# The opening modulation: weight pages become the stationary operand of the product

## The chip, the cores and the metric

The kernel runs on one core of a Trainium2 chip. The time is device microseconds of one execution, lower is better. Before the change three timed runs gave 2663.68, 2665.32 and 2666.12 us, so the median is 2665.32 us.

A core has TensorE (matrix products; PE in the profile, and PEld for its weight loads), VectorE (DVE), ScalarE (ACT), GpSimd (POOL) and SyncE (SP), whose queue issues the transfers between HBM and on-chip memory. A product on TensorE has a stationary operand, which a load brings into the array, and a moving operand, whose columns pass through it.

## The reference

One layer of a hybrid diffusion backbone works on 1024 latent tokens and 256 context tokens of width 1024. Each sublayer normalizes its tokens and modulates them with vectors that come from a conditioning vector through one weight matrix, `w_ada` (1024 x 9216). Latent tokens are conditioned on `c`, context tokens on `c_ctx`:

```python
mods   = split(silu(c) @ w_ada + b_ada, 9)
mods_c = split(silu(c_ctx)[None] @ w_ada + b_ada, 9)
h  = ffn_sublayer(h,  mods[0],   mods[1],   mods[2],   g_ffn1, w_ffn1_in, w_ffn1_out)
hc = ffn_sublayer(hc, mods_c[0], mods_c[1], mods_c[2], g_ffn1, w_ffn1_in, w_ffn1_out)

def ffn_sublayer(h, shift, scale, gate, g, w_in, w_out):
    hn = rmsnorm(h, g) * (1 + scale) + shift
    a, b = split(hn @ w_in, 2)
    return h + 0.5 * gate * ((silu(a) * b) @ w_out)
```

Behind these come the projections, a bidirectional mLSTM, a spatial gating unit, the merge, a second feed-forward sublayer for the latent tokens, and a last RMSNorm. The change touches only the first two modulations, shift and scale (columns 0 to 2047 of `w_ada`), for both conditions.

## The kernel before

Everything is kept transposed: features on the 128 partitions, tokens along the free dimension. Width 1024 is eight blocks of 128 features, called d. Big products use pairs of fp32r pages: a value is split into a rounded high part (a copy on ScalarE) and a residue (a subtraction on VectorE), and the product is made of three terms. `split` (L175) does this for weight pages. A product of plain fp32 operands appears in the trace as two loads and two matmuls.

The opening, up to about 51 us, works in this order. `ada_page` (L859) loads the 2048 columns of `w_ada` as sixteen pages of 512 KB: four quarters `qt` of 2 x 256 columns (shift and scale), with four pages `kp` each, and two blocks k of 128 inputs in each page. All transfers are issued on SyncE's queue, in the order of the loop from L938: the sixteen pages, with the two halves of the context tokens `hcp` after the second and the fourth, the first raw feed-forward page (`W.fetch`, tile `wraw`) after the fourteenth, three more raw pages at the end, then constants, and later eight more raw pages, which take the buffers of the pages of quarters 0 and 1, and the latent tokens (`h`).

`ada_mm` (L864) multiplies one page. The stationary operand is the conditioning (four columns: both conditions, as high parts and residues or with two zero columns) and the page moves, 512 columns at a time. Of every four blocks one goes as plain fp32 (L869), and three are split into `adhi` (ScalarE, L872) and `adlo` (VectorE, L874) and multiplied in two fp32r products (L875, L876). A quarter's result is a row of 512 values on four partitions; `ada_out` (L878) copies it and turns it into columns with four small fp32 products (L883), so that features lie on partitions. `ada_mods` (L886) adds the bias and makes scale factors.

Between the pages stand the sums of squares of the context tokens (`sums_c`, L962), the reciprocal root (`rstd_c`), its broadcast (`bcast_c`, L979), and per quarter `mod_a` (scale, tile `nt`, VectorE, L991) and `mod_b` (shift and split, tile `hnc`, ScalarE L996 and VectorE L997), which finish two of the eight blocks d of the modulated context tokens.

`tile0` (L1001) splits one raw feed-forward page into `hl`, and `proj_k` (L953) multiplies it with blocks of `hnc`, three fp32r matmuls of 256 columns for each block: 24 for a tile of 128 output features. The first three tiles are made in the opening, tile by tile as `hnc` gets ready; from L1076 a loop makes the remaining ones in pairs, gates them (`gate_c`) and stores them, while latent tokens are loaded and normalized in the background. `Weights` (L130) holds four split pages; `done` splits the next raw page and fetches another.

The order on TensorE, ScalarE and VectorE is fixed by hand: inside `inorder(last0)` each instruction is made to follow the one before it on its engine, and the loop that follows pins TensorE in the same way. Ten products of a page of ones (`WARM`, L1009) run before the first page is there.

Of the kernel before, what the change touches and what calls it, by code (L numbers as in the profile page):

```python
# [9 lines left out]
F32 = mybir.dt.float32  # L10
F32R = mybir.dt.float32r
# [27 lines left out]
NVEC = _o  # L39


WARM = 10
COST = lambda f: getattr(f, 'cost', 512)
MODG = lambda d: d % 2 == 0

# [12 lines left out]
def _build(ctx, tc, nc, a, out):  # L58
# [39 lines left out]
    def t2(name, dt=F32, shape=(128, 512)):  # L98
        return tp.tile(list(shape), dt, name=name, tag="t2", bufs=12)

    def mm_ps(name):
        return ps.tile([128, 512], F32, name=name, tag="mm", bufs=4)

    def sm_ps(name):
        return ps.tile([128, 512], F32, name=name, tag="sm", bufs=4)
# [679 lines left out]
    S.activation(sc2[:, 0, :], vs_("c"), AF.Silu)  # L785
    S.activation(sc2[:, 1, :], vs_("c_ctx"), AF.Silu)
    mods = cp.tile([128, 9, 2, 8], F32, name="mods")
    c4 = cp.tile([128, 8, 4], F32R, name="c4")
    cz = cp.tile([128, 16, 4], F32, name="cz")[:, :8]
    G.memset(cz, 0.0)  # L790
    ck = sc2.rearrange("p q k -> p k q")
    S.copy(c4[:, :, 0:2], ck)
    V.tensor_sub(c4[:, :, 2:4], ck, c4[:, :, 0:2].bitcast(F32))
    V.tensor_copy(cz[:, :, 0:2], ck)
    pick = t2("pick", shape=(4, 2))
    V.tensor_add(pick, ident[0:4, 0:2], ident[0:4, 2:4])

    def ada_load(page, m, hf, k):
        pgt = page()
# [54 lines left out]
    NQ = 4  # L854
# [4 lines left out]
    def ada_page(qt, kp):  # L859
        pg = hnp.tile([128, KP, 2, QW], F32, name="adapg", tag=f"pg{1 - qt // 2}", bufs=8)  # L860
        nc.sync.dma_start(pg.rearrange("p k m c -> p (k m c)"), a["w_ad0"][qt * (NKT // KP) + kp])
        return pg

    def ada_mm(pages, pr, kp):  # L864
        for j in range(KP):
            k = kp * KP + j
            src = pages[kp][:, j].rearrange("p m c -> p (m c)")
            if k % 4 == 0:
                T.matmul(pr[0:4, :], cz[:, k, :], src, start=k == 0, stop=False, skip_group_check=True)  # L869
                continue  # L870
            hi = t2("adhi", F32R)
            S.copy(hi, src)  # L872
            lo = t2("adlo", F32R)
            V.tensor_sub(lo, src, hi.bitcast(F32))  # L874
            T.matmul(pr[0:4, :], c4[:, k, :], hi, start=False, stop=False, skip_group_check=True)  # L875
            T.matmul(pr[0:2, :], c4[:, k, 0:2], lo, start=False, stop=k == NKT - 1, skip_group_check=True)  # L876

    def ada_out(qt, pr):  # L878
        row = t2("adrow", shape=(4, 2 * QW))
        S.copy(row, pr[0:4, :])  # L880
        pc = sm_ps("adc")
        for i in range(2 * QD):
            T.matmul(pc[:, 2 * i:2 * i + 2], row[:, i * 128:(i + 1) * 128], pick, start=True, stop=True)  # L883
        return pc

    def ada_mods(qt, pc):  # L886
        sl = slice(qt * QD, (qt + 1) * QD)
        bv = vs_("b_ada").rearrange("p (m d) -> p m d", m=9)
        for m in range(2):
            V.tensor_add(mods[:, m, :, sl],  # L890
                         pc[:, m * 2 * QD:(m + 1) * 2 * QD].rearrange("p (d q) -> p q d", q=2),
                         bv[:, m:m + 1, sl].to_broadcast([128, 2, QD]))
        V.scalar_tensor_tensor(smod[:, 0, :, sl], mods[:, 1, :, sl], 1.0,
                               vs_("g_ffn1")[:, sl].unsqueeze(1).to_broadcast([128, 2, QD]), ALU.add, ALU.mult)
# [43 lines left out]
    apg = [[] for _ in range(NQ)]  # L938
    for qt in range(NQ):
        for kp in range(NKT // KP):  # L940
            apg[qt].append(ada_page(qt, kp))
            if qt == 0 and kp % 2:
                i = kp // 2
                nc.sync.dma_start(hcp[i], a["cT"][4 * i:4 * i + 4].rearrange("d p t -> p d t"))
            if (qt, kp) == (3, 1):
                W.fetch(wfirst)
    for _ in range(3):
        W.fetch(wfirst)
    nc.sync.dma_start(cst[:, 1:], a["cst"].rearrange("p (a b) -> p a b", a=5)[:, 1:])
    nc.sync.dma_start(pos, a["pos"])  # L950
# [11 lines left out]
    def sums_c(p4, ds):  # L962
        for d in ds:
            sq = [t2("sq")[:, :256] for _ in range(2)]
            for i in range(2):
                S.activation(sq[i], hc[d + i], AF.Square)
            V.tensor_add(sq[0], sq[0], sq[1])
            for j in range(2):
                T.matmul(p4[:, j:j + 1], sq[0][:, j * 128:(j + 1) * 128], ones[:, 0:1], start=d == 0 and j == 0,
                         stop=d == NKT - 2, skip_group_check=True)  # L970

    def rstd_c(p4):
        y = rsqrt(p4[:, :2], 2, 1.0 / D)
        diag = t2("diag")
        for j in range(2):
            V.tensor_scalar(diag[:, j * 128:(j + 1) * 128], ident, y[:, j:j + 1], None, ALU.mult)
        return diag

    def bcast_c(diag):  # L979
        rb = sm_ps("rb")  # L980
        T.matmul(rb[:, :256], ones, diag[:, :256], start=True, stop=True)
        return rb[:, :256]
# [2 lines left out]
    nts = {}  # L985

    def mod_a(qt):
        ada_mods(qt, adc.pop(0))
        for d in range(qt * QD, (qt + 1) * QD):
            nts[d] = t2("nt")[:, :256]  # L990
            V.scalar_tensor_tensor(nts[d], hc[d], scc[:, d:d + 1], rsc, ALU.mult, ALU.mult)  # L991
# [9 lines left out]
    def tile0():  # L1001
        W.load()
        first.append(W.take("w1i", len(first)))
        pf.append(mm_ps("pa")[:, :256])

    last0 = {}
    with inorder(last0):
        wps = sm_ps("wps")
        for i in range(WARM):  # L1009
            T.matmul(wps[:, :128], ones, ones, start=True, stop=True)  # L1010
        pr = sm_ps("adr")
        for kp in range(4):
            ada_mm(apg[0], pr, kp)
        p4 = sm_ps("p4")
        sums_c(p4, (0, 2))
        for qt in range(1, NQ):
            pq, pr = pr, sm_ps("adr")
            ada_mm(apg[qt], pr, 0)
            if qt == 1:
                sums_c(p4, (4, 6))  # L1020
            elif qt == 2:
                mod_a(0)
            adc.append(ada_out(qt - 1, pq))
            ada_mm(apg[qt], pr, 1)
            if qt == 1:
                dg = rstd_c(p4)
            else:
                if qt == 2:
                    mod_b(0)
                mod_a(qt - 1)  # L1030
            ada_mm(apg[qt], pr, 2)
            if qt == 1:
                rb_ = bcast_c(dg)
            ada_mm(apg[qt], pr, 3)
            if qt == 1:
                S.copy(rsc, rb_)
            else:
                mod_b(qt - 1)
        tile0()
        proj_k(pf[0], first[0], range(4))  # L1040
        adc.append(ada_out(3, pr))
        tile0()
        proj_k(pf[0], first[0], (4, 5))
        mod_a(3)
        proj_k(pf[1], first[1], range(6))
        mod_b(3)
        tile0()
        proj_k(pf[0], first[0], (6, 7))
        proj_k(pf[1], first[1], (6, 7))
        W.load()  # L1050
        proj_k(pf[2], first[2], range(NKT))

    for _ in range(W.ahead):
        W.fetch(wraw)
    for i in range(3):
        W.done(wraw)

    n1 = [Norm(h[tb], 512, V) for tb in range(2)]
# [17 lines left out]
    for f in range(NF):  # L1076
        if f < NKT:
            for tb in range(2):
                nc.sync.dma_start(h[tb][f], a["xT"][f, :, tb * 512:(tb + 1) * 512])
        if 2 <= f < 2 + NKT:  # L1080
            for tb in range(2):
                slow(add_pos, tb, f - 2, cost=512, later=True)
                slow(n1[tb].sq, f - 2, cost=512, later=True)
                slow(nc.sync.dma_start, hsp[tb, f - 2], h[tb][f - 2], cost=0)
        if f == 2 + NKT:
            todo.extend([n1[0].rstd, n1[1].rstd] + [nop] * 12 + [n1[0].bcast, n1[1].bcast] + [nop] * 4)
            for d in range(4):
                slow(n1[0].inplace, d, s0, b0, cost=512, later=True)
                slow(A.F.early, fpage, 1, d, cost=512, later=True)
        if f == 12:  # L1090
            A.head()
        if f > 12:
            A.preload()
        if f == NF - 1:
            A.q.ring = lambda: hnpage(1, "ring0")
            for _ in range(HEAD):
                A.q.load()
            A.q.ring = A.ring
        if f:
            if f == 1:  # L1100
                pa = pf[2]
            else:
                pa = mm_ps("pa")[:, :256]
                proj(pa, W.take("w1i", 2 * f), hnc)
            gated()
            if f > 1:
                W.done(wraw)
            pb = mm_ps("pb")[:, :256]
            proj(pb, W.take("w1i", 2 * f + 1), hnc)
            W.done(wraw)  # L1110
        else:
            pa, pb = pf[0:2]
        gated = it(gate_c, f, pa, pb)
# [1164 lines left out]
```

## Time and profile before

| what | value |
|---|---|
| median of three timed runs | 2665.32 us (2663.68 to 2666.12) |
| profiled execution, its own time | 2660.64 us |
| span of its trace | 2658.8 us |
| TensorE busy | 2634.2 us, 99% of the span |
| mean granted TensorE clock | 0.998 |
| first modulation product starts | 5.85 us |
| last modulation product starts | 36.86 us |
| fifth projection tile starts | 51.19 us |

The trace is one execution on the chip. A line of the timeline gives start and length in microseconds, engine, line of the kernel, operation, output and inputs by the program's names, shape and count, and in brackets the idle time of the engine before it with what ended it. A line of the groups gives the busy time and the mean length of one. Matmuls are pipelined, so their lengths overlap, and the distance between starts is what a product costs. The granted clock is the share of full speed that TensorE was given.

### The profile page before, as it was taken

The page shows a single profiled execution, that of the slowest core. Times are in us where ns is not written, and L with a number is a line of the kernel's source. Part 1 is how long each engine was busy: PE and PEld are TensorE (multiplying, and loading weights), DVE is VectorE, ACT ScalarE, POOL GpSimd, SP SyncE. Part 2 cuts the span into 40 slices and gives each one's busy share as a digit, 9 for nine tenths or more (in the row PEclk, how much of TensorE's full clock was granted, in tenths as well). Part 3 has the DMA queues.
Part 4 walks back from the last instruction along what each step waited for, and adds up shares of the span by engine and source line. Part 5 has one row for each costly group of instructions (what it writes and reads, how often), then busy time and mean ns, then how long its engine had stood idle before and what let it go on. Part 6 is the DMA issues. An engine that isn't in the chain of part 4 may idle for free.

```text
span 2658.8 us, 35689 instructions
## 1 busy us (share of the span) xinstructions
PE 2634.2 (99%) x12766; PEld 2207.2 (83%) x12766; DVE 2018.3 (76%) x3633; ACT 1095.3 (41%) x1883; POOL 124.2 (5%) x211
## 2 busy tenths in 40 slices
PE   9999999999999999999999999999999999999998
PEld 6998888888889878888888888888887888888887
DVE  7889889788879647788774878677568877776855
ACT  6664333334346525554443342111345433334432
POOL 0000000000000000000000005342000000000000
PEclk9999999999999999999999999999999999999999
DMA  9923444369568122256553477448240433337545
GB/s 376 328 90 127 167 138 159 125 216 324 170 222 293 65 88 86 100 182 206 189 176 110 133 253 264 158 161 280 76 142 32 153 123 135 116 119 276 184 161 171
DMA packets 193090, 456.76 MB, mean 172 GB/s; under 512 B 20240, under 2 KB 40464, under 8 KB 192912
## 3 DMA queue, kind: packets, MB, share of 16 engines
q1 hardware_dynamic: 192912, 454.47, 50.4%
q8 instruction: 101, 1.65, 0.2%
q14 instruction: 77, 0.63, 0.1%
HBM read 328.95 MB, written 125.51 MB: 171 GB/s over the span
## 4 chain that ended last, share of the span: by engine, by line
PE 89%; DVE 5%; DMA 2%; issue 2%; ACT 1%; SPq 0%; POOL 0%; POOLq 0%; DVEq 0%; ACTq 0%
PE qb L431 20%; PE po L557 15%; PE pq L1427 13%; PE qa L431 10%; PE pt L1901 9%; PE pr L1338 6%; PE pb L206 2%; PE pc L1209 2%; PE pa L206 2%; PE pn L2014 2%; PE pu L1740 2%; PE pkc L1407 1%; PE pn L2012 1%; DVE ring L175 1%; PE pvc L1498 1%
## 5 line engine op out<-in xcount | busy, mean ns | idle before, releaser
L175 ACT CAST ring<-rawq 128x512 fp32r<-128x512 f32 x432 | 265.8, 620 | 533.2 <-PE qb L431 188.4
L557 PE MATMUL po<-gring,wring 128*128 128x512 f32 (+1 forms) x1896 | 425.0, 385 | 0.4 <-DMA gring<-fsp 0.4
L557 PEld LDWEIGHTS po<-gring,wring 128*128 128x128 f32 x1896 | 349.7, 188 | 71.5 <-issue 1.5
L175 DVE TENSOR_TENSOR ring<-rawq,ring 128x512 fp32r<-128x512 f32 x432 | 296.0, 689 | 131.5 <-ACT ring L175 130.1
L431 PE MATMUL qb<-fc,ring 128*128 128x512 f32 x1440 | 339.7, 390 | 0.1
L431 PEld LDWEIGHTS qb<-fc,ring 128*128 128x128 f32 x1440 | 270.2, 188 | 56.6 <-DVE u L452 0.8
L431 PE MATMUL qa<-fa,ring 128*128 128x512 f32 x1056 | 253.0, 390 | 0.0
L431 PEld LDWEIGHTS qa<-fa,ring 128*128 128x128 f32 x1056 | 198.2, 188 | 41.4 <-issue 0.5
L431 PE MATMUL qb<-fb,ring 128*128 128x512 f32 x984 | 229.8, 390 | 0.0
L431 PEld LDWEIGHTS qb<-fb,ring 128*128 128x128 f32 x984 | 184.7, 188 | 38.3
L1427 PE MATMUL pq<-fc,ring 128*128 128x512 f32 x864 | 211.1, 393 | 0.3 <-DVE py L1440 0.2
L1427 PEld LDWEIGHTS pq<-fc,ring 128*128 128x128 f32 x864 | 161.0, 188 | 33.8 <-DVE py L1440 1.4
L175 ACT CAST wring<-rw 128x512 fp32r<-128x512 f32 x154 | 95.9, 622 | 225.9 <-PE po L557 197.2
L1901 PE MATMUL pt<-yp,ring 128*128 128x512 f32 x768 | 184.3, 397 | 0.0
L175 DVE TENSOR_TENSOR wring<-rw,wring 128x512 fp32r<-128x512 f32 x154 | 105.6, 685 | 93.3 <-ACT wring L175 93.0
L1901 PEld LDWEIGHTS pt<-yp,ring 128*128 128x128 f32 x768 | 144.2, 188 | 29.2
L1427 PE MATMUL pq<-fa,ring 128*128 128x512 f32 x576 | 139.8, 391 | 0.0
L1427 PE MATMUL pq<-fb,ring 128*128 128x512 f32 x576 | 137.3, 393 | 0.0
L1427 PEld LDWEIGHTS pq<-fb,ring 128*128 128x128 f32 x576 | 107.7, 188 | 22.2 <-PE pu L1781 0.3
L1427 PEld LDWEIGHTS pq<-fa,ring 128*128 128x128 f32 x576 | 107.3, 188 | 21.8 <-DVE ring L175 0.2
L175 ACT CAST ring<-rawt 128x512 fp32r<-128x512 f32 x64 | 39.7, 620 | 187.6 <-PE pt L1901 177.5
L813 DVE SCALAR_TENSOR_TENSOR adacc<-adapg,sc,adacc 128x512 f32<-128x512 f32 x140 | 102.6, 745 | 8.3 <-DMA adapg<-in_w_ada_dram 7.5
(367 smaller groups left out, 4112.3 us busy)
## 6 DMA issues: line engine op xcount, KB each, us to landing
fsp<-fhl SPq DMA_DIRECT2D x66, 512.0 KB, 2.7
gring<-fsp SPq DMA_DIRECT2D x66, 512.0 KB, 3.4
adapg<-in_w_ada_dram SPq DMA_DIRECT2D x112, 256.0 KB, 3.5
wraw<-in_w1i_dram SPq DMA_DIRECT2D x44, 512.0 KB, 5.5
graw<-fsp SPq DMA_DIRECT2D x88, 256.0 KB, 3.4
rawq<-in_w1i_dram SPq DMA_DIRECT2D x38, 512.0 KB, 4.2
rawq<-in_w2i_dram SPq DMA_DIRECT2D x38, 512.0 KB, 3.3
fsp<-x SPq DMA_DIRECT2D x66, 256.0 KB, 2.0
```

The lines of the kernel that those rows point to most:

```text
L175: ins = S.copy(hl[:, 0, :], src).ins, V.tensor_sub(hl[:, 1, :], src, hl[:, 0, :].bitcast(F32)).ins
L206: T.matmul(pt, x, y, start=i == 0, stop=i == n - 1)
L431: T.matmul(pt, hl[:, x, sl], pages[p][k][:, y, :], start=first and i == 0, stop=i == 11, skip_group_check=not first)
L557: T.matmul(pt[:, cs], w[:, x, sl], g[:, y, cs], start=grp and kp == 0 and i == 0, stop=kp == NFP - 1 and i == 2, skip_group_check=not grp)
L813: eng.scalar_tensor_tensor(acc, pgt, sc2[:, q, k:k + 1], acc, ALU.mult, ALU.add)
L1209: T.matmul(pt, hl[d // 4][:, x, sl], g[:, y, :], start=f == 0 and d % 2 == 0 and i == 0, stop=f == NF - 1 and i == 2, skip_group_check=True)
L1338: T.matmul(self.pt[m], pg[:, x, sl], hl[:, y, :], start=first and k == 0 and i == 0, stop=k == 3 and i == 2, skip_group_check=not first)
L1407: T.matmul(self.cp[:, o:o + 256], hl[:, x, k * 128:(k + 1) * 128], hnc[kc][:, y, :], start=p == 1 and k == 0 and i == 0, stop=p in (2, 4) ...
L1427: T.matmul(pt, hl[:, x, k * 128:(k + 1) * 128], pg[k][:, y, :], start=first and k == 0 and i == 0, stop=k == 3 and i == 2, skip_group_chec ...
L1740: T.matmul(pu[:, 0:257], ksl[:, kt * 128:(kt + 1) * 128], wv, start=True, stop=True)
L1901: T.matmul(pt, hl[:, x, k * 128:(k + 1) * 128], pg[:, y, :], start=kh + k + i == 0, stop=kh == 1 and k == 3 and i == 2)
L2014: T.matmul(pn[:, 0:257], qi[:, c_, :], self.C[d][:, c_, :], start=False, stop=c_ == 1)
```

## The change

The operands change places. Each 128 x 128 block of a page, in plain fp32, is now the stationary operand, and the conditioning moves: both conditions and thirty columns of zeros, 32 columns. The result comes out with features on partitions, so the row copy and the turning products go, as do the splits of the pages. A quarter makes 32 products (eight blocks k, four blocks of output features), which accumulate in one PSUM tile.

The order changes with it. Token halves are loaded ahead of the first and the second page, and one raw feed-forward page after every quarter. The sums of squares run within quarter 0, the modulation of a quarter follows it at once and is followed by a `tile0`; projection columns (`cols`) stand after the second page of quarters 1, 2 and 3, and a fourth tile is made in the opening. The warm-up has sixteen products instead of ten. A spare tile `gap_` takes the place of a removed one.

```diff
-WARM = 10
+WARM = 16
...
-    c4 = cp.tile([128, 8, 4], F32R, name="c4")
-    cz = cp.tile([128, 16, 4], F32, name="cz")[:, :8]
+    gap_ = cp.tile([128, 32], F32, name="gap_")
+    cz = t2("cz")[:, 0:256].rearrange("p (k n) -> p k n", k=8)
     G.memset(cz, 0.0)
-    ck = sc2.rearrange("p q k -> p k q")
-    S.copy(c4[:, :, 0:2], ck)
-    V.tensor_sub(c4[:, :, 2:4], ck, c4[:, :, 0:2].bitcast(F32))
-    V.tensor_copy(cz[:, :, 0:2], ck)
-    pick = t2("pick", shape=(4, 2))
-    V.tensor_add(pick, ident[0:4, 0:2], ident[0:4, 2:4])
+    V.tensor_copy(cz[:, :, 0:2], sc2.rearrange("p q k -> p k q"))
...
-    def ada_mm(pages, pr, kp):
+    NC = 32
+
+    def ada_mm(qt, kp, pr):
         for j in range(KP):
             k = kp * KP + j
-            src = pages[kp][:, j].rearrange("p m c -> p (m c)")
-            if k % 4 == 0:
-                T.matmul(pr[0:4, :], cz[:, k, :], src, start=k == 0, stop=False, skip_group_check=True)
-                continue
-            hi = t2("adhi", F32R)
-            S.copy(hi, src)
-            lo = t2("adlo", F32R)
-            V.tensor_sub(lo, src, hi.bitcast(F32))
-            T.matmul(pr[0:4, :], c4[:, k, :], hi, start=False, stop=False, skip_group_check=True)
-            T.matmul(pr[0:2, :], c4[:, k, 0:2], lo, start=False, stop=k == NKT - 1, skip_group_check=True)
-
-    def ada_out(qt, pr):
...
+            for i in range(2 * QD):
+                m, d = divmod(i, QD)
+                T.matmul(pr[:, NC * i:NC * i + NC], apg[qt][kp][:, j, m, d * 128:(d + 1) * 128], cz[:, k, 0:NC],
+                         start=k + i == 0, stop=k == NKT - 1, skip_group_check=True)
...
     for qt in range(NQ):
         for kp in range(NKT // KP):
+            if qt == 0 and kp < 2:
+                nc.sync.dma_start(hcp[kp], a["cT"][4 * kp:4 * kp + 4].rearrange("d p t -> p d t"))
             apg[qt].append(ada_page(qt, kp))
-            if qt == 0 and kp % 2:
-                i = kp // 2
-                nc.sync.dma_start(hcp[i], a["cT"][4 * i:4 * i + 4].rearrange("d p t -> p d t"))
-            if (qt, kp) == (3, 1):
-                W.fetch(wfirst)
-    for _ in range(3):
         W.fetch(wfirst)
...
+        for qt in range(NQ):
+            adc.append(sm_ps("adc"))
+            for kp in range(4):
+                ada_mm(qt, kp, adc[qt])
+                if (qt, kp) == (0, 0):
+                    p4 = sm_ps("p4")
+                    sums_c(p4, (0, 2))
+                elif (qt, kp) == (0, 1):
+                    sums_c(p4, (4, 6))
+                    dg = rstd_c(p4)
+                elif (qt, kp) == (0, 3):
+                    S.copy(rsc, bcast_c(dg))
+                    mod_a(0)
+                    mod_b(0)
+                    tile0()
+                elif (qt, kp) == (1, 1):
+                    cols(0, 0, 1)
+                elif (qt, kp) == (2, 1):
+                    cols(0, 2, 3)
+                    cols(1, 0, 1, 2, 3)
+                elif (qt, kp) == (3, 1):
+                    cols(2, 0, 1, 2, 3)
+            if qt:
+                mod_a(qt)
+                mod_b(qt)
+                tile0()
+        for i in range(3):
+            cols(i, 4, 5)
+        for i in range(3):
+            cols(i, 6, 7)
+        cols(3, *range(NKT))
...
-    for i in range(3):
+    for i in range(4):
         W.done(wraw)
...
             if f == 1:
-                pa = pf[2]
+                pa, pb = pf[2:4]
+                gated()
```

More of the change, by code (lines that the diff above doesn't have):

```diff
@@ L862, in ada_page @@
         return pg
-    def ada_mm(pages, pr, kp):
+    NC = 32
+    def ada_mm(qt, kp, pr):
         for j in range(KP):
             k = kp * KP + j
-            src = pages[kp][:, j].rearrange("p m c -> p (m c)")
-            if k % 4 == 0:
-                T.matmul(pr[0:4, :], cz[:, k, :], src, start=k == 0, stop=False, skip_group_check=True)
-                continue
-            hi = t2("adhi", F32R)
-            S.copy(hi, src)
-            lo = t2("adlo", F32R)
-            V.tensor_sub(lo, src, hi.bitcast(F32))
-            T.matmul(pr[0:4, :], c4[:, k, :], hi, start=False, stop=False, skip_group_check=True)
-            T.matmul(pr[0:2, :], c4[:, k, 0:2], lo, start=False, stop=k == NKT - 1, skip_group_check=True)
-    def ada_out(qt, pr):
[L879 to L884, printed above, removed]
+            for i in range(2 * QD):
+                m, d = divmod(i, QD)
+                T.matmul(pr[:, NC * i:NC * i + NC], apg[qt][kp][:, j, m, d * 128:(d + 1) * 128], cz[:, k, 0:NC],
+                         start=k + i == 0, stop=k == NKT - 1, skip_group_check=True)
     def ada_mods(qt, pc):
@@ L890, in ada_mods @@
             V.tensor_add(mods[:, m, :, sl],
-                         pc[:, m * 2 * QD:(m + 1) * 2 * QD].rearrange("p (d q) -> p q d", q=2),
+                         pc[:, m * NC * QD:(m + 1) * NC * QD].rearrange("p (d q) -> p q d", q=NC)[:, 0:2, :],
                          bv[:, m:m + 1, sl].to_broadcast([128, 2, QD]))
@@ L987, in mod_a @@
     def mod_a(qt):
-        ada_mods(qt, adc.pop(0))
+        ada_mods(qt, adc[qt])
         for d in range(qt * QD, (qt + 1) * QD):
@@ L1004, in tile0, with cols @@
         pf.append(mm_ps("pa")[:, :256])
+    def cols(i, *ks):
+        proj_k(pf[i], first[i], ks)
     last0 = {}
@@ L1010, in _build @@
             T.matmul(wps[:, :128], ones, ones, start=True, stop=True)
[L1011 to L1028, printed above, removed]
-                    mod_b(0)
[L1030 to L1051, printed above, removed]
+        for qt in range(NQ):
[11 more added lines that the diff above has]
+                    mod_a(0)
+                    mod_b(0)
+                    tile0()
[10 more added lines that the diff above has]
+                tile0()
@@ L1104, in _build @@
                 proj(pa, W.take("w1i", 2 * f), hnc)
-            gated()
-            if f > 1:
+                gated()
                 W.done(wraw)
-            pb = mm_ps("pb")[:, :256]
-            proj(pb, W.take("w1i", 2 * f + 1), hnc)
-            W.done(wraw)
+                pb = mm_ps("pb")[:, :256]
+                proj(pb, W.take("w1i", 2 * f + 1), hnc)
+                W.done(wraw)
         else:
```

## The prediction

> **What bounds the kernel now.** I read the page's busy table first, then the chain of waits over the first 100 us, then TensorE's timeline and the stage table of that stretch, and last the groups by shape and the queue's issues.
>
> ```profile
> span 2658.8 us, 35689 instructions
> PE 2634.2 (99%) x12766; PEld 2207.2 (83%) x12766; DVE 2018.3 (76%) x3633; ACT 1095.3 (41%) x1883; POOL 124.2 (5%) x211
> ```
>
> TensorE is busy over the whole span, so time can only move where its work or its waits change: the opening. The profiled execution took 2660.64 us, 1.84 us more than its span; the median of the timed runs is 2665.32 us, 4.7 us above it. I make the sum in the profile's time and add the difference it gives to the median.
>
> TensorE's timeline of the opening (start, length, instructions, and what ended an idle time):
>
> ```profile
> 0.97 4.03 PE L1010 MATMUL wps<-ones 128*128 128x128 f32 x20 [0.97 <-POOL epst L88]
> 5.85 1.02 PE L869 MATMUL adr<-adapg,cz 128*4 128x512 f32 x2 [0.85 <-DMA adapg<-in_w_ad_dram]
> ...
> 13.47 1.20 PE L969 MATMUL p<-ones,sq 128*128 128x1 f32 x8
> ...
> 18.41 1.05 PE L883 MATMUL adc<-pick,adrow 4*128 4x2 f32 x8
> ...
> 29.54 0.40 PE L876 MATMUL adr<-adlo,c 128*2 128x512 f32 x1 [0.98 <-DVE adlo L874]
> 29.77 0.40 PE L875 MATMUL adr<-adhi,c 128*4 128x512 f32 x1
> ...
> 31.06 1.02 PE L869 MATMUL adr<-adapg,cz 128*4 128x512 f32 x2
> 32.01 0.40 PE L875 MATMUL adr<-adhi,c 128*4 128x512 f32 x1
> ...
> 36.86 0.40 PE L876 MATMUL adr<-adlo,c 128*2 128x512 f32 x1
> ...
> 38.79 1.45 PE L957 MATMUL pa<-hnc,hl 128*128 128x256 f32 x10 [1.30 <-DVE hl L175]
> ...
> 48.35 3.00 PE L206 MATMUL pb<-hnc,hl 128*128 128x256 f32 x24
> 51.19 3.00 PE L206 MATMUL pa<-hnc,hl 128*128 128x256 f32 x24
> ```
>
> The first page is used at 5.85, the last modulation product starts at 36.86, and 51.19 is my mark: there the fourth projection tile of the context tokens is done and the fifth starts. From then on tile follows tile every 2.84 us (51.19 - 48.35) with no idle time, before and after the change alike. What the change is worth is how far this mark moves.
>
> Who paces the stretch up to 36.86 is in the groups of the first 52 us (count, busy us, mean ns, idle before) and in the transfer rates:
>
> ```profile
> L874 DVE TENSOR_TENSOR adlo<-adapg,adhi 128x512 fp32r<-128x512 f32 x24 | 15.6, 687 | 7.7 <-ACT adhi L872 7.7
> L872 ACT CAST adhi<-adapg 128x512 fp32r<-128x512 f32 x24 | 13.7, 614 | 6.0 <-DMA adapg<-in_w_ad_dram 5.9
> L175 DVE TENSOR_TENSOR hl<-wraw,hl 128x1024 fp32r<-128x1024 f32 x7 | 8.3, 1222 | 0.6 <-ACT hl L175 0.5
> L175 ACT CAST hl<-wraw 128x1024 fp32r<-128x1024 f32 x8 | 8.2, 1043 | 2.5 <-issue 1.2 <-PE pa L957 1.2
> L991 DVE SCALAR_TENSOR_TENSOR nt<-hc,smod,rsc 128x256 f32<-128x256 f32 x8 | 3.5, 482 | 0.2
> L997 DVE SCALAR_TENSOR_TENSOR hnc<-nt,mods,hnc 128x256 fp32r<-128x256 f32 x8 | 3.5, 479 | 0.2 <-ACT hnc L996 0.2
> L996 ACT ACTIVATE hnc<-nt,mods 128x256 fp32r<-128x256 f32 x8 | 3.6, 501 | 4.5 <-DVE nt L991 4.5
> L890 DVE TENSOR_TENSOR mods<-adc,vec 128x4 f32<-128x4 f32 x8 | 0.9, 155 | 1.2 <-PE adc L883 1.2
> L893 DVE SCALAR_TENSOR_TENSOR smod<-mods,vec 128x4 f32<-128x4 f32 x4 | 0.7, 165 | 0.1
> L1036 ACT COPY rsc<-rb 128x256 f32<-128x256 f32 x1 | 0.4, 372 | 3.5 <-PE rb L981 3.5
> ```
>
> ```profile
> 20.00:30.00 10.00, 8.96 (x34) 2.55 (x31) 9.00 (x26) 6.38 (x13) 0.00 (x0) 1.00 1.03 406
> ```
>
> Transfers run full at 406 GB/s, so a 512 KB page lands every 1.29 us (524288 / 406), and a quarter of four pages 5.2 us after the last. TensorE's products, the splits on VectorE (15.6 us) and the arrivals share the bound; none holds alone.
>
> **The change, part by part.** *Removed:* 24 splits on ScalarE and 24 on VectorE (13.7 and 15.6 us), four row copies, and TensorE's narrow products. Per quarter TensorE had two fp32 products at 0.95 us (31.06 to 32.01), twelve fp32r ones at 0.23 (29.54 to 29.77) and the eight turning instructions: 1.9 + 2.8 + 1.0 = 5.7 us, 22.7 for four. ScalarE and VectorE are not the bound afterwards, so their relief counts only through shorter waits.
>
> *Added:* per quarter 8 x 4 = 32 fp32 products, and an fp32 product is two loads and two matmuls (the ten warm-up products are x20): 64 pairs a quarter, 256 in all, each with a 128-column weight load and 32 moving columns. The trace has no such stream, but it has the same load with fewer and with more moving columns:
>
> ```profile
> 18.41 0.96 PEld L883 LDWEIGHTS adc<-pick,adrow 4*128 4x128 f32 x8
> 4.28 0.41 PEld L1010 LDWEIGHTS wps<-ones 128*128 128x128 f32 x3
> ```
>
> One load lasts 0.19 us and they overlap: (0.96 - 0.19) / 7 = 0.110 us with 2 moving columns, (0.41 - 0.19) / 2 = 0.11 with 128. So 32 columns cost the load's pace. From above: the eight turning instructions took 18.41 to 19.39, 0.123 each with a fill at the front. I take 0.111, as streams are long: 28.4 us, with ends 28.2 and 31.5. That is 5.8 us **more** TensorE work than the 22.7 removed.
>
> *Other TensorE work up to the mark, unchanged in amount:* sums 16 x 0.111 = 1.8, the broadcast (an fp32 product of 256 columns, half of 0.95) 0.5, four tiles x 2.84 = 11.4. Together 28.4 + 1.8 + 0.5 + 11.4 = 42.1 us.
>
> *Moved transfers:* the first half of the tokens now stands ahead of page 0, which is then used at 5.85 + 1.29 = 7.1. Six more warm-up products (twelve pairs at 0.11, 1.3 us) end near 6.3, under that wait; without the cover they would cost 1.3. The sixteen pages with two token halves and three raw pages between them put page 15 at 5.85 + 20 x 1.29 = 31.7, while TensorE asks for it after 40: transfers stop being a bound. Raw pages arrive every quarter, ahead of their use. Behind them the queue holds the next eight raw pages, which reuse the buffers of quarters 0 and 1:
>
> ```profile
> 26.77 8.86 SPq L147 DMA_DIRECT2D wraw<-in_w1i_dram  x8
> ```
>
> They start at 26.77 with the queue full; quarter 1 now frees its buffers at about 25, so nothing gets later, nor do the token loads behind them.
>
> *Waits, new ones included.* TensorE runs in the written order, so everything behind a waiting projection column waits with it, the next pages' products above all. After a quarter comes a chain over ScalarE and VectorE: modulation 2 x 0.155 + 0.165 = 0.5, nt 2 x 0.48, the last bias on ScalarE 0.5, residues 2 x 0.48, and then a raw page's split on VectorE, 1.2 (its ScalarE half, 1.0, runs beside the residues): 4.1 us. In its place TensorE has two pages of the next quarter, 32 x 0.111 = 3.6 us, and in quarter 2 six columns more (0.7). The first chain is longer by the broadcast's copy (0.4). So the first column waits about 1.0, the second 0.2, the third 0.8; at the end the columns 4 and 5 of three tiles (18 x 0.118 = 2.1 us) cover most of the last 2.6 us to columns 6 and 7, 0.5 left. With 0.2 of start-up: 2.7 us.
>
> *Sum.* 7.1 + 42.1 + 2.7 = 51.9 against 51.19: **+0.7 us**. Bounds: no waits at all and the cheap pair, 49.0 (-2.2); the dear pair and twice the waits, 57.7 (+6.5). Hence 2661.3 in the profile's time, and 2665.32 + 0.7, about **2666 us**: TensorE exchanges waits for work, one for one. A measurement of this kernel tells about 0.2% from no change, 5.3 us.
>
> **The rivals.** *Slower: the clock is halved under the narrow products.* The stage table in steps of the clock's windows (length, then busy time and count of PE, PEld, DVE, ACT, POOL, then granted clock):
>
> ```profile
> 7.64:11.05 3.41, 2.58 (x7) 0.43 (x7) 1.85 (x3) 1.19 (x3) 0.00 (x0) 1.00 1.03 391
> 11.05:14.46 3.41, 2.88 (x14) 1.29 (x13) 2.19 (x5) 2.88 (x7) 0.00 (x0) 1.00 1.05 399
> 14.46:17.88 3.42, 3.42 (x10) 1.30 (x10) 2.53 (x5) 3.29 (x9) 0.00 (x0) 0.50 1.04 413
> 28.12:31.53 3.41, 2.43 (x9) 0.43 (x8) 3.41 (x8) 1.72 (x4) 0.00 (x0) 1.00 1.01 395
> 977.02:980.44 3.42, 3.42 (x32) 3.26 (x29) 0.00 (x0) 0.36 (x1) 0.00 (x0) 1.00 0.00 0
> 980.44:983.85 3.41, 3.41 (x21) 3.02 (x22) 0.60 (x3) 2.41 (x5) 0.00 (x0) 1.00 0.00 0
> ```
>
> From 14.46 to 17.88 the clock was 0.50. The window ahead was busier by the profile (2.88) than 28.12 to 31.53 (2.43), which was followed by full clock. The difference is what it was busy with: eight of its 14 matmuls had one moving column (the L969 row), and the others moved 512, the first of them mostly before the window: 5 x 0.23 = 1.15 us of 3.41, 34%. The other window had six of these and half an fp32 product, 1.9 us, 54%. If the gate counts moving columns, the new stream gives 32 / 512 x 0.475 = 0.03 us in each 0.111, 27%, and falls below. At half clock a load stream runs at 0.213:
>
> ```profile
> 2.20 2.13 PE L1010 MATMUL wps<-ones 128*128 128x128 f32 x9
> ```
>
> (2.13 - 0.42) / 8. All 256 pairs there cost 256 x 0.102 = +26 us; the projection columns between quarters fill a window each and reopen the clock for the next, so half to three quarters of that, less the waits it swallows: +12 to +20, 2677 to 2686, about 2681. It decides as soon as two of the sixteen pages' worth of windows in each quarter are halved (4 x 2 x 1.6 = 13 us). Against it: apart from its wide matmuls and eight loads (0.9 us) that window was empty for 1.4 us, which the dense stream is not; the window at 977.02, whose second half held sixteen of the matmuls below with 16 columns each, was not followed by half clock; and 32 columns with their way through the array keep it occupied longer than one column does. A single event can't settle it.
>
> ```profile
> 978.59 2.40 PE L1606 MATMUL pgt<-gpg,grow 32*128 32x16 f32 x20
> ```
>
> [...]
>
> *Faster: the timed runs lose more to the gate than the profiled one.* They are 4.7 us longer, and a window at half clock costs up to 1.7 us. If three such windows fall on the old opening and none on the new, 2665.3 + 0.7 - 5.1 is 2661, with shorter waits 2660. For it: the one halved window shows that the old opening can lose this way. Against it: nothing shows where the 4.7 us lie, and TensorE there waited for splits anyway.
>
> *Faster: the change doesn't cost what it says, one load serving both matmuls.* Then 128 x 0.111 = 14.2 us fall away and the transfers bind: page 15 at 31.7, 0.9 of products, 2.6 of chain, 18 columns and a tile (5.0), some waiting: 42 to 44, about 2657. Against it: every fp32 group here has as many loads as matmuls.
>
> **How the numbers follow.** Forecast (within the bounds -2.2 to +6.5) 0.46; halved clock 0.36; timed runs' gate 0.12; single load 0.06. The forecast's own range is 2662 to 2671. Both signs matter, so the range reaches into the slower case up to 2684 and down to 2659, leaving out the worst of the halved clock and half of the single load. Of the forecast's 0.46, 0.40 lies within 5.3 us, 0.04 above and 0.02 below. Faster: 0.02 + 0.06 + 0.12 x 0.7 = 0.16, and 0.02 for causes that I don't see, 0.18. Slower: 0.36 + 0.04 = 0.40, less 0.02 for a halved clock that hides under waits, 0.38. Same: 0.44.
>
> **What would show each step.** Loads of the new products 0.11 us apart and a granted clock of 1.00 from 7 to 45 us carry the forecast; 0.21 apart and clock 0.50 there, the first rival. The first new product near 7.1; last page landed near 32 with its use ten microseconds later; three waits of a projection column on the split of a raw page, each about 1 us or less; the fifth tile starting near 51.9. The prediction is wrong if the clock falls, if a pair takes another time than 0.111, or if the fifth tile starts where I say and the time differs all the same: then the cause lies behind the opening, where I cost everything at nothing because TensorE is already without idle time there.

## The result, and the profile after

The changed kernel took 2684.89 us (median of four runs, 2679.76 to 2690.25), the kernel before 2665.10 us beside it: a ratio of 1.0075 with a 95% interval of 1.0049 to 1.0100, so 0.5 to 1.0% slower. The forecast was 2666 us; the first rival, the halved clock, had said 2677 to 2686.

The page of the changed kernel begins:

```profile
span 2688.5 us, 35956 instructions
PE 2669.3 (99%) x12938; PEld 2257.8 (84%) x12938; DVE 2003.6 (75%) x3607; ACT 1080.5 (40%) x1854; POOL 124.7 (5%) x211
```

TensorE is as full as before, with 172 matmuls more, and VectorE and ScalarE have become lighter by about 15 us each. None of that tells why the span is 29.7 us longer. The chain that ended last, over the opening, does (start, length, engine, tile, line, count):

```profile
7.50 1.71 PE adc L866 x16
9.21 0.87 PE p L948 x8
10.07 3.37 PE adc L866 x16
13.44 1.66 PE p L948 x8
15.10 6.88 PE adc L866 x32
21.97 1.01 PE rb L960 x2
22.99 6.67 PE adc L866 x32
29.65 1.44 PE pa L936 x6
31.09 13.49 PE adc L866 x64
44.59 3.62 PE pa L936 x18
48.20 10.82 PE adc L866 x64
59.02 2.72 PE pa L936 x12
61.74 6.67 PE adc L866 x32
68.41 8.63 PE pa L936 x60
```

In this stretch the chain is TensorE alone, with no wait in it. The first page of modulation products takes 1.71 us for 16 pairs, 0.107 each; the second page takes 3.37 us, 0.211 each, and so it goes on. TensorE's timeline gives the two marks:

```profile
7.34 1.87 PE L866 MATMUL adc<-cz,adapg 128*128 128x32 f32 x16
76.87 3.00 PE L206 MATMUL pa<-hnc,hl 128*128 128x256 f32 x24
```

The fifth tile starts at 76.87 us instead of 51.19: 25.7 of the 29.7 us are lost in the opening. The stage table shows with what (length, busy time and count of PE, PEld, DVE, ACT, POOL, granted clock, transfer share, GB/s):

```profile
10.00:20.00 10.00, 10.00 (x49) 10.00 (x48) 2.55 (x14) 0.00 (x0) 0.00 (x0) 0.50 1.03 408
...
6.65:10.06 3.41, 3.41 (x34) 3.41 (x32) 1.29 (x4) 1.73 (x6) 0.00 (x0) 1.00 1.07 399
10.06:13.47 3.41, 3.41 (x19) 3.41 (x18) 0.23 (x1) 0.00 (x0) 0.00 (x0) 0.50 1.02 408
...
44.19:47.61 3.42, 3.42 (x17) 3.42 (x18) 0.00 (x0) 0.00 (x0) 0.00 (x0) 0.50 1.03 379
47.61:51.02 3.41, 3.41 (x33) 3.41 (x32) 0.00 (x0) 0.00 (x0) 0.00 (x0) 1.00 1.06 389
51.02:54.43 3.41, 3.41 (x19) 3.41 (x18) 1.95 (x7) 1.22 (x3) 0.00 (x0) 0.50 0.63 234
...
61.26:64.67 3.41, 3.41 (x19) 3.41 (x17) 0.00 (x0) 0.00 (x0) 0.00 (x0) 0.50 0.00 0
...
1006.75:1010.16 3.41, 3.41 (x30) 3.25 (x29) 0.44 (x3) 0.37 (x3) 0.00 (x0) 1.00 0.00 0
1010.16:1013.58 3.42, 3.42 (x11) 2.74 (x11) 0.16 (x2) 3.36 (x6) 0.00 (x0) 0.50 0.00 0
...
1607.50:1610.91 3.41, 3.33 (x15) 3.35 (x16) 2.75 (x5) 2.70 (x5) 0.00 (x0) 0.50 0.84 279
```

From 10 to 20 us TensorE is busy for all of its time, at half its clock. The lower rows are cut on the grid of the trace's clock records, which in the opening last 3.41 us or a multiple of it (10.06 to 47.61 is eleven times that); a step of 3.41 us is called a window here. The clock closed (went to half) at 10.06, opened (went to full) at 47.61 behind a window filled with projection columns (the 44.59 piece of the chain), closed again after one window of modulation products, and did not open at 61.26, although projection columns filled 2.2 us of the window ahead (2.4 by the timeline, where they start at 58.83). It opened at 71.50 and was at 1.00 from there to 1010.16. The remaining 4.0 us lie behind the opening: the last rows show two windows there at half clock, and each can lose, by estimate, up to half of its 3.41 us.

### The profile page after: what moved, and what is told of

Its sections match the earlier page's. It is cut to its first block, busy times and chain, and to the rows that moved or that the text cites. A ratio compares the mean times of both kernels' runs of the same rounds, so it can differ in the third digit from the quotient of the medians.

```text
span 2688.5 us, 35956 instructions
## 1 busy us (share of the span) xinstructions
PE 2669.3 (99%) x12938; PEld 2257.8 (84%) x12938; DVE 2003.6 (75%) x3607; ACT 1080.5 (40%) x1854; POOL 124.7 (5%) x211
## 4 chain that ended last, share of the span: by engine, by line
PE 87%; DVE 6%; DMA 3%; issue 2%; ACT 1%; POOL 0%; SPq 0%; POOLq 0%; DVEq 0%; ACTq 0%
PE qb L431 19%; PE po L557 13%; PE pq L1399 12%; PE qa L431 10%; PE pt L1873 9%; PE pr L1310 6%; PE pb L206 2%; PE pc L1181 2%; PE pa L206 2%; PE adc L866 2%; PE pn L1986 2%; PE pu L1712 2%; DVE ring L175 1%; PE pkc L1379 1%; PE pn L1984 1%
```

## The experiments

The question is whether the clock is the cause or goes with another one, and what it answers to. Each kernel is timed beside the kernel before on the same chip; the median of the kernel before was 2665.10 us beside the changed kernel, 2660.97 beside the next four and 2662.23 beside the last four. So the ratios and the fifth tile can be compared down the table, the times only roughly.

| kernel | moving columns | fifth tile starts, us | time, us | ratio to before (95%) |
|---|---|---|---|---|
| changed | 32 | 76.87 | 2684.89 | 1.0075 (1.0049 to 1.0100) |
| 128 columns | 128 | 50.73 | 2658.40 | 0.9994 (0.9985 to 1.0003) |
| 64 columns | 64 | 64.76 | 2673.52 | 1.0052 (1.0036 to 1.0069) |
| old kernel, new order of transfers | - | 51.72 | 2662.62 | 1.0006 (0.9997 to 1.0016) |
| 2 columns | 2 | 78.28 | 2685.75 | one run |
| 64 columns, wide sums | 64 | 50.83 | 2660.95 | 0.9996 (0.9987 to 1.0006) |
| 96 columns | 96 | 51.26 | 2658.14 | one run |
| 64 columns, filled with ones | 64 | 66.17 | 2673.57 | one run |
| 128 columns, tighter order | 128 | 49.56 | 2656.93 | 0.9983 (0.9974 to 0.9992) |

### 128 moving columns

```diff
-    NC = 32
+    NC = 128
```

The conditioning then fills two tiles of zeros instead of half a one; loads, matmuls and order stay.

> The changed kernel with 128 moving columns (both conditions and 126 zero columns) instead of 32; loads, matmuls and order stay. Theory A, the clock gate counts the time in which columns move: 128 columns in two passes take 0.107 us of the 0.111 between loads, so the granted clock stays 1.00 from the first page on, loads stand 0.11 us apart, the fifth tile starts at 52 us instead of 77, and the time is 2663 to 2668 us, about 20 less than the changed kernel. Theory B, the order and its waits are what costs and the half clock only goes with them: the fifth tile stays near 77 us and the time near 2685. Theory C, the gate looks at the work done in the array, which zeros don't cause: clock 0.50 as before, 2685.

TensorE's timeline of this kernel:

```profile
7.16 2.00 PE L867 MATMUL adc<-cz,adapg 128*128 128x128 f32 x16
...
20.07 0.48 PE L937 MATMUL pa<-hnc,hl 128*128 128x256 f32 x2
20.86 0.74 PE L937 MATMUL pa<-hnc,hl 128*128 128x256 f32 x4 [0.30 <-DVE hl L175]
21.44 7.31 PE L867 MATMUL adc<-cz,adapg 128*128 128x128 f32 x64
...
37.76 0.48 PE L937 MATMUL pa<-hnc,hl 128*128 128x256 f32 x2
38.61 1.45 PE L937 MATMUL pa<-hnc,hl 128*128 128x256 f32 x10 [0.37 <-DVE hl L175]
39.90 3.73 PE L867 MATMUL adc<-cz,adapg 128*128 128x128 f32 x32
...
50.73 3.00 PE L206 MATMUL pa<-hnc,hl 128*128 128x256 f32 x24
```

The stage from the first new product to the fifth tile, as a row of the stage table:

```profile
7.00:51.00 44.00, 43.33 (x376) 42.80 (x376) 20.26 (x51) 12.43 (x23) 0.00 (x0) 1.00 1.03 403
```

Four times as many columns, nearly all of them zeros, and the opening is 26.1 us shorter: 64 pairs take 7.31 us where the 32-column kernel took 13.49. The clock is 1.00 from the first page on. What Theory A forecast for the clock came true; B and C fall. The 0.107 us in which it has 128 columns move is my estimate, which no run shows by itself: the runs show the pace of the pairs, 0.107 us with 32 columns at full clock (1.71 us for 16) and 0.110 with 128 (21.44 to 28.50 for 64). By the prediction's price, 0.475 us for 512, the 128 columns come to 0.119, so by either estimate they fill a pair's time. The fifth tile came 1.3 us earlier than I expected, as only two waits of projection columns are left, with 0.30 and 0.37 us of idle time. Against the kernel before there is no difference that the runs could tell. That also gives the size of the change without the loss of clock: an exchange of waits for work, about even. Columns moved and columns written aren't separated by any run: a product here writes as many as it moves.

### 64 moving columns

```diff
-    NC = 32
+    NC = 64
```

> The changed kernel with 64 moving columns. Theory A with the closing level between the windows seen (34% of a window with moving columns was followed by half clock, 46% not): 64 columns move for 0.053 of 0.107 us, 50%, so full clock, the fifth tile at 52 us, 2663 to 2668 us. If the level lies above 50%, as a gate that counts something else would have it: half clock from the second window on, fifth tile at 70 to 77 us, 2680 to 2690.

Neither expectation came true. The stage table, cut at the clock's steps:

```profile
10.15:13.56 3.41, 3.41 (x32) 3.41 (x32) 0.81 (x5) 0.00 (x0) 0.00 (x0) 1.00 1.02 406
13.56:16.98 3.42, 3.42 (x18) 3.42 (x18) 1.64 (x10) 0.00 (x0) 0.00 (x0) 0.50 1.03 404
40.87:44.28 3.41, 3.41 (x18) 3.41 (x18) 0.00 (x0) 0.00 (x0) 0.00 (x0) 0.50 1.00 391
44.28:47.70 3.42, 3.42 (x33) 3.42 (x32) 0.00 (x0) 0.00 (x0) 0.00 (x0) 1.00 1.05 389
47.70:51.11 3.41, 3.41 (x33) 3.41 (x33) 2.16 (x7) 1.57 (x3) 0.00 (x0) 1.00 1.05 387
```

The clock closed at 13.56, one window later than with 32 columns, opened at 44.28 and stayed open, with the same 64-column products that had not opened it for 30 us. A pair with 128 columns takes 0.11 us (the 7.31 us row), so by estimate 64 columns move for about half of the time and 32 for about a quarter. With products alone, at one half, the clock was at 1.00 behind a window at 1.00 (47.70 to 51.11), and at 0.50 behind windows at 0.50 (64 pairs took 13.51 us from 27.78 on, 0.211 each). The timeline shows what the window ahead of 13.56 held besides them:

```profile
9.98 1.98 PE L866 MATMUL adc<-cz,adapg 128*128 128x64 f32 x16
11.80 1.00 PE L948 MATMUL p<-ones,sq 128*128 128x1 f32 x8
12.66 6.26 PE L866 MATMUL adc<-cz,adapg 128*128 128x64 f32 x32
```

Products from 10.15 to 11.80 and from 12.66 to 13.56, 2.55 us, and one-column sums between them: a moving share, by estimate, of 2.55 x 0.5 / 3.41 = 37%. For the changed kernel's window ahead of 10.06 it is 0.7 us of warm-up and 1.7 us of products at a quarter, 33%; for the old kernel's weak window the prediction had 34%.

### The old kernel with the new order of transfers

```diff
         for kp in range(NKT // KP):
+            if qt == 0 and kp < 2:
+                nc.sync.dma_start(hcp[kp], ...)
             apg[qt].append(ada_page(qt, kp))
-            if qt == 0 and kp % 2:
-                ...
-            if (qt, kp) == (3, 1):
-                W.fetch(wfirst)
-    for _ in range(3):
         W.fetch(wfirst)
```

> The kernel before with the new order of transfers alone: token halves ahead of pages 0 and 1, one raw page after every quarter. Theory A (the transfers are no part of the loss): the first page comes 1.3 us later and later pages up to 3.9 us later by the raw pages between them, of which the splits hide some: 0 to +4 us, 2665 to 2669. Rival (the new order of transfers starves the opening): +10 us or more.

```profile
7.17 1.02 PE L869 MATMUL adr<-adapg,cz 128*4 128x512 f32 x2 [1.56 <-DMA adapg<-in_w_ad_dram]
...
51.72 1.47 PE L206 MATMUL pa<-hnc,hl 128*128 128x256 f32 x11
...
5.89:9.30 3.41, 1.68 (x4) 0.28 (x4) 0.69 (x1) 0.62 (x1) 0.00 (x0) 1.00 1.05 383
9.30:12.71 3.41, 1.89 (x6) 0.34 (x6) 1.97 (x3) 2.09 (x4) 0.00 (x0) 1.00 1.02 408
```

The first page comes 1.3 us later, the fifth tile 0.5, and the time is level. The transfers are no part of the loss, as Theory A had it. The 0.5 is a net figure: the opening of the old kernel had one window at half clock, and this one shows none (each of its fp32 products of 512 columns takes 0.95 to 0.96 us from start to start, against 1.80 in that window), which can hide up to 1.7 us by estimate, half of 3.41.

The last two rows also say something on the clock. TensorE was busy for only about half of these windows, but with 512 columns a product, and the clock stayed open (behind them, from 12.15 to 13.10, an fp32 product took 0.95 us). By the prediction's prices, 0.23 us for an fp32r product and 0.475 for each half of an fp32 one, columns moved for about 1.4 and 1.5 of 3.41 us, 41% and 43%. So, as far as such estimates go, full clock followed at 41% and 43% here, and half clock at 37% above.

### 2 moving columns

```diff
-    NC = 32
+    NC = 2
```

> The changed kernel with the two conditions alone moving, no zero columns. Theory A: columns move for under 2% of the time, clock 0.50 over the whole modulation as with 32, loads 0.213 us apart, fifth tile at 75 to 80 us, 2680 to 2691; the thirty zero columns bought nothing. Rival (thirty columns do keep the clock part of the time): the fifth tile 3 us or more later than with 32.

The fifth tile starts at 78.28 us, 1.4 later than with 32, and the time of 2685.75 us lies among those of the 32-column kernel. That kernel's clock opened once in between, at 47.61, where a stretch of projection columns happened to fill the window ahead (from 44.40 on); that the thirty zero columns bought this isn't shown. The stage table of the 2-column kernel also has a window with more projection columns, behind which the clock was not open:

```profile
42.15:45.56 3.41, 3.41 (x17) 3.41 (x18) 0.00 (x0) 0.00 (x0) 0.00 (x0) 0.50 1.03 389
45.56:48.98 3.42, 3.42 (x19) 3.42 (x18) 0.00 (x0) 0.00 (x0) 0.00 (x0) 0.50 1.05 386
```

Projection columns ran from 42.78 on, 2.8 us of the first window, and yet the second is still at half.

### 64 columns and wide sums

```diff
-    NC = 32
+    NC = 64
...
-                T.matmul(p4[:, j:j + 1], sq[0][...], ones[:, 0:1], ...)
+                T.matmul(p4[:, 64 * j:64 * j + 64], sq[0][...], ones[:, 0:64], ...)
```

> The changed kernel with 64 moving columns, and the sums of squares of the context tokens made with 64 moving columns (of ones) instead of 1; their extra columns are read by nobody. Theory A: with 64 columns the clock closed at 13.56 us because the window ahead of it held the one-column sums and its moving share was about 35%, while windows of 48% at full clock, later in the same run, were not closed. With wide sums every window has 48% or more: clock 1.00 throughout, fifth tile at 51 us, time 13 us below the kernel with 64 columns, level with the kernel before. Rival (50% is too little by itself and only luck of the windows' place kept it open later): clock 0.50 from the second or third window on, fifth tile beyond 60 us.

```profile
9.10 1.06 PE L948 MATMUL p<-ones,sq 128*128 128x64 f32 x8
...
11.80 1.06 PE L948 MATMUL p<-ones,sq 128*128 128x64 f32 x8
...
50.83 3.00 PE L206 MATMUL pa<-hnc,hl 128*128 128x256 f32 x24
...
9.27:12.69 3.42, 3.42 (x32) 3.42 (x32) 0.85 (x2) 0.73 (x3) 0.00 (x0) 1.00 1.02 408
```

The last row is the stage table's for a window with wide sums. The clock stays at 1.00 (four windows from 5.86 to 19.51 have it, and from 21.62 and 30.90 on 64 pairs take 7.06 and 7.06 us), the fifth tile starts 13.9 us earlier than in the 64-column kernel, and the ratio to the kernel before goes from 1.0052 to 0.9996, for 16 matmuls that were made wider and not one more or less. By estimate columns moved for about half of the window in the last row, and full clock followed; in the 64-column kernel the window at 37% was followed by half clock.

### 96 columns

```diff
-    NC = 32
+    NC = 96
```

> The changed kernel with 96 moving columns. Theory A: moving share 72% in the product stream and about 50% in the window with the one-column sums, above the closing level of 35 to 46%: full clock, fifth tile at 51 us, a span like that with 128 columns. If the level of the windows with sums is what decides and lies above 50%: a half clock from the second or third window on, and a span 10 us longer or more.

Full clock (1.00 in the three windows from 6.80 to 17.04; from 22.01 and 31.29 on 64 pairs take 7.07 and 7.06 us), fifth tile at 51.26 us, a span of 2656.3 us: as Theory A had it. The window with the one-column sums (10.21 to 13.63) has products for about 2.4 of 3.42 us here, at three quarters: about 53% by estimate, and the next window was at 1.00.

### 64 columns filled with ones

```diff
-    G.memset(cz, 0.0)
+    G.memset(cz, 1.0)
...
-    NC = 32
+    NC = 64
```

> The changed kernel with 64 moving columns, the 62 filler columns ones instead of zeros; only the two conditions' columns are read. Theory A (the gate counts time in which columns move, whatever they hold): like 64 zero-filled columns, half clock from the window with the one-column sums until a window filled with projection columns, fifth tile at 58 to 70 us. Theory C (the gate looks at switching in the array): full clock from the first page on, fifth tile at 51 us.

```profile
9.30:12.71 3.41, 3.41 (x32) 3.41 (x32) 0.85 (x3) 0.51 (x2) 0.00 (x0) 1.00 1.03 410
12.71:16.12 3.41, 3.41 (x19) 3.41 (x18) 2.19 (x13) 0.00 (x0) 0.00 (x0) 0.50 1.04 410
```

The clock closes in the same way, here after a window with a moving share of about 31% by estimate, and the fifth tile starts at 66.17 us. With ones as with zeros the window behind the one-column sums was at 0.50; other contents were not tried. The clock opened again at about 46.84 us, one window later than with zeros, as the grid of windows and the pace of the products from 45.67 on (64 pairs in 7.63 us) give it: the window ahead held projection columns for 2.2 us (43.43 to 45.67) and 64-column products for the remaining 1.2, by estimate a moving share of about 83%.

### 128 columns in a tighter order

```diff
-    NC = 32
+    NC = 128
...
-            if qt == 0 and kp < 2:
-                nc.sync.dma_start(hcp[kp], ...)
             apg[qt].append(ada_page(qt, kp))
+            if qt == 0 and kp in (1, 2):
+                i = kp - 1
+                nc.sync.dma_start(hcp[i], ...)
...
-                if (qt, kp) == (0, 0):
+                if (qt, kp) == (0, 2):
                     p4 = sm_ps("p4")
                     sums_c(p4, (0, 2))
-                elif (qt, kp) == (0, 1):
+                elif (qt, kp) == (0, 3):
                     sums_c(p4, (4, 6))
                     dg = rstd_c(p4)
-                elif (qt, kp) == (0, 3):
+                elif (qt, kp) == (1, 1):
                     S.copy(rsc, bcast_c(dg))
...
-                elif (qt, kp) == (1, 1):
+                elif (qt, kp) == (2, 1):
                     cols(0, 0, 1)
-                elif (qt, kp) == (2, 1):
+                elif (qt, kp) == (3, 1):
                     cols(0, 2, 3)
                     cols(1, 0, 1, 2, 3)
-                elif (qt, kp) == (3, 1):
+                elif (qt, kp) == (3, 2):
                     cols(2, 0, 1, 2, 3)
```

> 128 moving columns, and three things in the order: pages 0 and 1 loaded ahead of the token halves, the sums of squares after pages 2 and 3 of quarter 0, and the projection columns one or two pages later. Theory (with a full clock TensorE's own work sets the end of the opening): TensorE starts 1.3 us earlier, the waits of projection columns (0.3 and 0.4 us with 128 columns) go, the fifth tile starts at 49 us instead of 50.7, the time is 1 to 2 us below that with 128 columns, 0.998 of the kernel before. Rival (the first page's arrival is hidden anyway): fifth tile at 50.5 us, the time that of 128 columns.

```profile
0.97 6.01 PE L994 MATMUL wps<-ones 128*128 128x128 f32 x32 [0.97 <-POOL ones L86]
6.82 5.53 PE L867 MATMUL adc<-cz,adapg 128*128 128x128 f32 x48
...
49.56 3.00 PE L206 MATMUL pa<-hnc,hl 128*128 128x256 f32 x24
```

No wait is left, and the fifth tile starts at 49.56 us. TensorE started only 0.3 us earlier, not 1.3: now the sixteen warm-up products, which end at 6.8, stand in the way of the first page. With a ratio of 0.9983 (0.9974 to 0.9992) this version is a little faster than the kernel before, and by the two ratios 0.9% faster than the changed one. Its interval overlaps that of the 128 columns in the changed order (0.9985 to 1.0003), so what the order alone is worth shows in the trace, 1.2 us at the mark, and not in the times.

## Why the prediction was wrong, by its own steps

**Added work: right, at full clock.** A pair of the new products takes 0.107 us there (16 in 1.71) against 0.111 in the sum, and about 0.11 with 128 columns (64 pairs in 7.31, the length of the last one included). What the removed products were worth by themselves no run shows.

**Moved transfers: right, but for the cover.** The first new product started at 7.34 us against 7.1. The warm-up was to end at 6.3 and ran until the first new product: the trace's first clock record, at 1.00, starts at 6.65 instead of 4.22, and ahead of it the pairs were 0.213 us apart (five in 1.27 from 4.33 on, the last lasting 0.42), near the 0.211 measured at 0.50. The last page landed at 32.96 us against 31.7, long before its use. The order of transfers made the old kernel's opening 0.5 us longer, net of the half window that this run was spared.

**Waits: mechanism right, too large.** With 128 columns two were left, 0.30 and 0.37 us of idle time. By the distance between starts they cost about twice that: six matmuls of projection columns took 1.37 us (20.07 to 21.44) and twelve took 2.14 (37.76 to 39.90), 0.66 and 0.72 more than 0.118 each. With 0.3 in the two other groups that is 1.7 us against 2.7 in the sum, so the fifth tile came at 50.7 instead of 51.9.

**The clock: this step failed.** The forecast priced all 256 new pairs at the full clock, 0.111 us each, and set 0.36 on the rival. Measured, the pairs took 49.6 us instead of 28.4, most of them at a granted clock of 0.50 and 0.211 us. None of the three reasons against the rival bore out. That the old weak window had been empty for 1.4 us did not matter: the new windows were busy for 3.41 of 3.41 us and the clock closed all the same (1.00 from 6.65 to 10.06, 0.50 from there on). The stretch of 16-column matmuls at 978 us had been cut in two by a step of the clock. In the changed kernel the same stretch falls into one window, 1006.75 to 1010.16, and the next one is at half; in the old kernel with the new order of transfers it falls, by the grid of windows, into 978.69 to 982.10, and the mean clock from 980 to 986 is 0.72, as one window at half gives it. The third, that 32 columns on their way occupy the array for longer than one (a matmul lasted 276 ns with 32 and 250 with one at full clock, as the profile models the lengths), didn't help: the clock closed as it does with 2 columns, where the fifth tile is only 1.4 us later. The moving share that the rival had worked out from two rows orders, by estimate, every closing that these runs show in the opening.

**The rival's price: the median fell within its span, the trace above it.** It took half to three quarters of the 26 us for the pairs, since projection columns would open the clock after each quarter. From the chain, the pairs took 1.71 + 3.37 + 6.88 + 6.67 + 13.49 + 10.82 + 6.67 = 49.6 us against 28.4, so 21.2 us more, above three quarters: one of three stretches of columns opened the clock, for one window. And it left out that the columns run at the low clock too: 16.4 us against 11.4. With 1.2 for sums and broadcast and 0.2 at the start, less the 2.7 of waits that are gone, that is 25 us over the forecast's 51.9. The median is only 19.8 us above the kernel before: the trace is of the longest of the four runs, 5.4 us above their median, and the trace before is of a run 4.5 us below its own. So that the median lies inside the rival's +12 to +20 is partly luck.

**Behind the opening** I costed nothing, and within a window or two that holds. Of the two half windows there the first is in the old kernel with the new order of transfers too, at the same stretch of its work (mean clock 0.72 from 980 to 986), so it does not belong to the new products as such; for the second that isn't shown. The mean granted clock over the whole span was 0.999 with 96 and with 128 columns, against 0.986 in the changed kernel.

## What to carry to other kernels

Where small moving operands pass through large stationary ones, look at the granted clock before costing the stream at full clock, and work out for what share of the time columns move. By that estimate, with a pair's 0.11 us as the time of 128 columns, the stream at a quarter ran mostly at 0.50 here (32 columns, 49.6 us for 256 pairs), at one half it was at 0.50 from 13.56 to 44.28 and at 1.00 from there on in the opening (64 columns), and at three quarters and with 128 columns at 1.00. Padding with zero columns up to the pace of the loads cost next to nothing (0.107 us a pair with 32 columns, about 0.11 with 128). A rival that follows from two rows of the profile should not be outvoted by "TensorE isn't idle": a busy column of 3.41 in 3.41 us looked the same at both clocks. Look at the granted clock in steps of its own window (3.41 us in these traces), and at short narrow stretches that another start time could put into one window, as the 16-column matmuls at 1007.18 here.

## What the runs showed of the hardware that was not expected

Every row above that is cut on the grid of the windows has a granted clock of 1.00 or 0.50. The moving shares here are estimates from the timelines, each of a single window of these kernels. At 1.00, windows at 37% and 31% (64 columns), 33% (32 columns) and 34% (the old kernel) were followed by 0.50; windows at 41% and 43% (the old kernel with the new order of transfers) and at about one half were followed by 1.00. One window behind the opening doesn't fit that order, as far as estimates so close can be told apart: in the changed kernel the 128-column products lasted for 1.43 of 3.41 us, 42% (1604.09 to 1607.50, the lengths as the profile models them), and 0.50 followed. At 0.50, the 64-column products, at one half, were not followed by 1.00 for 30 us (13.56 to 44.28), nor were windows with 2.4 and 2.8 us of projection columns and narrow products beside them (32 and 2 columns). Windows nearly filled with projection columns were followed by 1.00 (44.19 to 47.61 and 68.09 to 71.50 with 32 columns, 40.87 to 44.28 with 64), and so was one with 2.2 us of them and 64-column products in the rest (64 columns of ones). The share alone doesn't order these: in the old kernel a window that was about three quarters filled with wide matmuls (14.46 to 17.88) was followed by full clock, while the one with 2.8 us of projection columns, about 82%, was not.
